# Eight small edits to the step order of a hybrid decoder layer on one core

## The chip, the core and the metric

The kernel runs on one core of a Trainium2 chip. The metric is the device time of one execution in microseconds; of several executions the median is taken. All data is float32. Matmuls run on pairs of "fp32r" tiles: every operand is split into a rounded high part and a remainder, and three products (high·high, high·low, low·high) are summed.

## What is computed

A decoder layer with five branches on 2048 tokens of width 1024, and 256 memory tokens:

```
h    = rms_norm(x, norm_g)
proj = h @ w_in                                  # (2048,1024) @ (1024,4652)
ya = spatial_gating(u, v, ...)                   # A: chunks of 128 tokens
yb = forgetting_attention(q, k, v, f, ...)       # B ("fox"): causal, QK-norm, 4 heads of 64
yc = mlstm(qk, v, i, f, o, ...)                  # C: chunkwise matrix memory, 16 chunks
yd = rwkv7_time_mix(token_shift(pd), ...)        # D: delta rule, 8 blocks of 256 tokens here
ym = memory_attention(q, rms_norm(mem) @ w_kv)   # M: cross-attention, QK-norm
out = x + concat(y * silu(z) for the five) @ w_out   # (2048,1280) @ (1280,1024)
```

## The kernel before, in words

Tokens go in four quarters of 512 (Q = 512, NQ = 4). The weight columns come in blocks of 256 (`Dk`, `Bq`, `Mq`, ...), and one block of one quarter is 48 matmuls of 512 columns or 96 of 256 columns, the three products counted. A block goes through `proj_T` (matmul line 267), `proj_T2` (line 289), `proj_tok2` (line 301) or `proj_tok` (line 315).

**Phase one** (lines 453 to 609): for each quarter the RWKV columns k, narrow, r, v, z. **Phase two** (lines 612 to 694): first the memory queries of the last quarter (`group_M`: block `Mq`, then its gate `Mz`), then for each quarter five mLSTM blocks (`Cqk0`, `Cv`, `Cqk1`, `Co`, `Cz`) and four fox blocks. **Phase three** (lines 756 to 816): blocks `Av`, `Au`, `Az`, the memory's keys and values, and `Mq`, `Mz` of the other quarters, while the attention runs beside them. **Phase four** (lines 819 to 886): the output projection by quarters (matmul line 879).

**Steps and lanes.** All work that is not a projection is written as Python generators that stop at `yield`. `tick()` (line 200) is called some eight times per block; it moves the weight loader on by a step, moves every evacuation in the crowd `evac` on by one step, and moves each of the five lanes on by its rate in steps (`RATES`, line 32: gate 0.4, mlstm 0.8, front 1.0, back 1.33, fox 1.815). `lane.drain()` and `evac.drain()` run what is left without any projection between the steps. So a `yield` more between two instructions puts one tick more, that is six matmuls of 512 columns or twelve of 256, between them in the order of the program.

The order of the program is a priority and not the order itself: a scheduler at build time lays out each engine's queue, takes the earliest instruction of the program that is ready by its own estimates, and may take later ones first where the earlier are not ready. On the chip each engine then follows its queue.

What the change touches:

- `Rwkv.front` (line 1255), one generator for each of the 8 blocks: norm and decay. It yields `2 + LATER` times (line 1316) between the reciprocal norms `rn` (DVE, `rsqrt`, lines 152 to 156) and PE's use of them (line 1322), and as often (line 1334) between the product `th` (POOL, line 1333) and its matmul (line 1338). `Rwkv.back` (line 1343) is the recurrence, one generator of 62 steps for each block, whose outcome `output` (line 1505) is stepped from the next block's `back`. A `front` waits until the output of the block before the last is out.
- `head_norm` and `qk_post` (lines 394 to 421): the QK-norm of two tiles of 128 tokens; the scaled tile `yn` (DVE, line 413) is transposed by PE (line 418) one yield later. `qk_cols` allows two of these at a time and the tile `yn` has two buffers.
- `low_rank` (line 1218): splits the low-rank weights of RWKV, with eight masks on POOL (line 1231). It is added to `evac` in quarter 0 beside block k.
- `group_M` (line 657) and the end of phase one (lines 607 to 609). The weights of the next block are fetched when a block begins (`W`, `prefetch`, `load_w`, lines 206 to 258): four tiles of 256 KB into the pool `stage["pool"]`, which is `dp` with three buffers in phase one and `sp` with two in phase two; the two pools share their memory, so that `sp` begins when `dp` is free. The lane `gate` (`gate_prep`, line 1525) gets its work at the start of phase two; it prepares the gates of branches B and C in a chain of small transfers through memory, and is drained behind `group_M`.
- `Attention.run` and `Unit` (lines 932 to 1178): 16 fox units (4 heads by 4 quarters) and 16 memory units. `maxima` finds a bound of the scores for the unit after the next; its outcome `mm` (line 1020) goes through PE (line 1069) three yields later. `average` runs `nkt` tiles of scores, exponentials `pe` (line 1087, 6 buffers) and products into `acc` (line 1108), the products three steps behind the scores, in `nkt + 3` steps. `run` spreads the steps of `maxima` over those of `average` by the ratio `per`. `finish` (line 1125) reads `acc`, which has one buffer, in the steps of the next unit.

The end of phase three in the code:

```
    while att.done < NH * (NQ + 1):
        fox.step()
    att.c5.close()
...
    while len(wo) < NK:
        load_wo()
        for _ in range(1):
            fox.step()
    fox.rate = 1.0
    for q in range(NQ):
        while att.ended < (NQ + q + 1) * NH:
            fox.step()
```

Of the kernel before, what the change touches and what calls it, by code (L numbers as in the profile page):

```python
# [18 lines left out]
P = 128  # L19
# [8 lines left out]
EPS = 1e-6  # L28
Q = 512
NQ = S // Q  # L30
LATER = 3
RATES = dict(gate=0.4, mlstm=0.8, front=1.0, back=1.33, fox=1.815)
PACE = (3, 1, 7)
EH = 0.6065306597126334
# [86 lines left out]
def body(ctx: ExitStack, tc, x, xT, mem, memT, wp, wkv, wout, pv, wa, sguT, sgub, out, dbg=None):  # L121
# [78 lines left out]
    def tick():  # L200
        step_w()
        evac.tick()
        for l in lanes.values():
            l.tick()

    def load_w(parts, src, ncol=256):

# [201 lines left out]
    def qk_post(y, scale, d):  # L409

        r = yield from head_norm(y, 512, EPS)
        y3 = y.rearrange("q (u x) -> q u x", x=HD)
        V.tensor_tensor(y3, y3, r, op=ALU.mult)
        yield
        pt = bank()
        for p in range(2):
            for ii in range(2):
                T.transpose(pt[:, (2 * p + ii) * P:(2 * p + ii + 1) * P], y[:, ii * 256 + p * P:ii * 256 + (p + 1) * P], ident)
        A.activation(y, pt, AF.Copy, scale=scale)
        yield  # L420
        SY.dma_start(d.rearrange("p q t -> q p t"), y.rearrange("q (p t) -> q p t", p=2))
# [19 lines left out]
    def tok_cols(wt, hts, i, d):  # L441


        def post(pt):
            o = xp.tile([P, 512], F32, tag="gl", name="tok")
            A.copy(o, pt)
            yield FREE
            SY.dma_start(d, o.rearrange("q (i x) -> q i x", x=256))

        evac.add(post(proj_tok(wt, hts, i)), "gl")  # L450


    with ExitStack() as c1:
# [72 lines left out]
        for q in range(NQ):  # L526
# [60 lines left out]
            for nm, j in (("k", 2), (None, 8), ("r", 0), ("v", 4), ("z", 6)):  # L587
                if not nm:
                    evac.add(narrow(proj_narrow(W("narrow"), hts), tok))
                    continue  # L590
                wt = W("D" + nm)
                if nm == "r" and q + 1 < NQ:
                    rows(q + 1, [("xt", 3)] * 3)
                pts = None
                if nm == "k" and not q:
                    pts = proj_T2(wt, hts)
                    evac.add(keep(xrs, rb0))
                    evac.add(rwkv.low_rank())
                if nm == "z":
                    pts = proj_T2(wt, hts, send(norm_x(q + 1), "norm_g", Q) if q + 1 < NQ else None)  # L600
                for p in range(2):
                    evac.add(shifted(pts[p] if pts else proj_T(wt, p, hts), j + p, (store_gate if nm == "z" else store)(dd[nm][p, :, tok])))
# [3 lines left out]
                lanes["back"].q.append(rwkv.back(2 * q + b))  # L606
        while ahead and next(ahead[-1][2], ahead) is not ahead:
            pass
        evac.drain()


    csp = cw.enter_context(ExitStack())
# [44 lines left out]
    def group_M(q, then=None):  # L657

        tok = slice(q * Q, (q + 1) * Q)
        qk_cols(W("Mq"), hts, hp2[:, 15:16], lambda i: qkd["Mq"][:, :, q * Q + i * P:q * Q + (i + 2) * P])  # L660
        wt = W("Mz")
        gate_cols(wt, hts, [gzd["M"][p, :, tok] for p in range(2)], proj_T2(wt, hts, then) if then else None)

# [225 lines left out]
class Attention:  # L889
# [42 lines left out]
    def run(self, units, ahead=2):  # L932
        mlane, flane = Lane(), Lane()
        for n in range(-ahead, len(units)):
            m = units[n + ahead] if n + ahead < len(units) else None
            if m:
                mlane.q.append(m.load())
                mlane.q.append(m.maxima())
            if n < 0:
                while mlane.q:  # L940
                    mlane.step()
                    yield
                continue
            u = units[n]
            done, per = 0, (m.nkt + 8) / (u.nkt + 3) if m else 0
            for k, _ in enumerate(u.average()):
                while done < (k + 1) * per:
                    mlane.step()
                    done += 1
                flane.step()  # L950
                self.end()
                yield
            mlane.drain()
            flane.drain()
            self.done = n + 1
            flane.q.append(u.finish())
        while flane.q or self.tails:
            flane.step()
            self.end()
            yield  # L960


class Unit:
# [66 lines left out]
    def maxima(self):  # L1030
# [31 lines left out]
        mm = fp.tile([P, 4, 4], F32R, tag="mm", name="mm")  # L1062
        A.copy(mm[:, :, 0:2], att.minus.to_broadcast([P, 4, 2]))
        self.split4(mx[:, :, 0], mm[:, :, 2:4])
        for _ in range(3):
            yield
        pm = att.bank()
        for i in range(4):
# [3 lines left out]
    def weights(self, kt):  # L1072
# [10 lines left out]
        if diag:  # L1083
            T.matmul(p2[:, f:f + P], att.identr, att.masks[0], start=False, stop=False)
        T.matmul(p2[:, f:], ka[:, ks], self.qb[:, f:], start=False, stop=True)  # L1085
        e = fp.tile([P, Q], F32, tag="pe", bufs=6, name="pe")
        A.activation(e[:, f:], p2[:, f:], AF.Exp)  # L1087
        return kt, f, e

# [20 lines left out]
    def average(self):  # L1110
        self.acc = self.att.bank("acc")
        late, pair = deque(), []
        for kt in range(self.nkt + 3):
            if kt < self.nkt:
                late.append(self.weights(kt))
            if 0 < kt <= self.nkt:
                self.rest(*late[-1 if kt == self.nkt else -2])
            if kt > 2:
                pair.append(late.popleft())
                if len(pair) == 2:  # L1120
                    self.product(pair)
                    pair = []
            yield
# [631 lines left out]
```

## Time and profile before

| what | us |
|---|---|
| median of 3 runs | 1740.68 |
| lowest of the runs | 1735.09 |
| the profiled execution, its own time | 1736.49 |
| its span, first to last instruction | 1734.8 |
| PE (TensorE, matmul) busy in the span | 1641.8 (95%) |
| DVE (VectorE) busy | 1196.9 (69%) |
| ACT (ScalarE) busy | 881.3 (51%) |
| POOL (GpSimd) busy | 302.3 (17%) |

The mean granted clock of TensorE in the span is 0.975 of full speed. PE's time is that of pipelined matmuls whose ends are modelled, so that "busy" holds slow matmuls too; idle time is the sure part. Times within the span are counted from its first instruction.

### The profile page before, as it was taken

To read this page: it belongs to the slowest core of one execution; us is meant where nothing else is said; L and a number is where in the kernel's file an instruction comes from. 1 tells how busy PE (TensorE), PEld (TensorE's weight loads), DVE (VectorE), ACT (ScalarE), POOL (GpSimd) and SP (SyncE) were. 2 spreads that over 40 slices of the span, in tenths; PEclk is the share of its full clock that TensorE was granted. 3 is DMA by queue.
4 is the path that set the end of the run, shared out by engine and by line. 5 is a ranking of instruction groups with operands and counts; after the bars stand their busy time and mean duration, and the time that the engine had idled before them with its cause. 6 is when DMAs were issued, how large, how long until landed. Compare 5 with 4: busy or idle time off the path is not lost.

```text
span 1734.8 us, 31669 instructions
## 1 busy us (share of the span) xinstructions
PE 1641.8 (95%) x11306; PEld 1282.2 (74%) x11306; DVE 1196.9 (69%) x2990; ACT 881.3 (51%) x1895; POOL 302.3 (17%) x356
## 2 busy tenths in 40 slices
PE   7898999799999999999999999999999988999999
PEld 5676778687978888798888766667656655677887
DVE  7678685685977679488676887788687786752220
ACT  5566554544555455555444756566465646631110
POOL 5010000010100101010000045344444242100000
PEclk9999999899999999999999989999999999999999
DMA  6878654542453443344334544334334425654441
GB/s 198 256 230 259 184 161 97 139 145 86 135 157 101 132 141 115 86 134 146 98 101 141 167 120 130 105 102 130 96 86 110 113 68 137 191 162 114 143 130 56
DMA packets 200151, 234.36 MB, mean 135 GB/s; under 512 B 75016, under 2 KB 107336, under 8 KB 199992
## 3 DMA queue, kind: packets, MB, share of 16 engines
q1 hardware_dynamic: 185144, 218.69, 43.7%
q10 hardware_dynamic: 14848, 13.64, 2.6%
q8 instruction: 89, 1.46, 0.4%
q14 instruction: 70, 0.57, 0.1%
HBM read 180.44 MB, written 51.81 MB: 134 GB/s over the span
## 4 chain that ended last, share of the span: by engine, by line
PE 64%; DVE 16%; DMA 11%; ACT 4%; issue 3%; POOL 1%; SPq 1%; ACTq 0%; DVEq 0%; POOLq 0%
PE pj L315 14%; PE pj L879 12%; PE pj L267 12%; PE acc L1108 4%; DMA wraw<-in_wp 4%; PE pj L289 4%; DVE wt L225 2%; PE wk L1026 2%; PE p L1082 2%; PE p L1085 2%; PE rw L1359 1%; PE rw L1482 1%; PE rw L1484 1%; DVE ht L330 1%; DVE mx L1040 1%
## 5 line engine op out<-in xcount | busy, mean ns | idle before, releaser
L267 PE MATMUL pj<-ht,wt 128*128 128x512 f32 x1632 | 422.6, 403 | 5.8 <-DVE ht L330 2.7
L267 PEld LDWEIGHTS pj<-ht,wt 128*128 128x128 f32 x1632 | 298.3, 190 | 84.5 <-issue 10.5
L315 PE MATMUL pj<-wt,ht 128*128 128x256 f32 x2400 | 332.7, 290 | 9.3 <-ACT wt L222 3.4
L315 PEld LDWEIGHTS pj<-wt,ht 128*128 128x128 f32 x2400 | 304.9, 193 | 27.5 <-issue 7.4
L225 DVE TENSOR_TENSOR wt<-wraw,wt 128x512 fp32r<-128x512 f32 (+1 forms) x312 | 217.6, 700 | 78.0 <-ACT wt L222 76.4
L222 ACT CAST wt<-wraw 128x512 fp32r<-128x512 f32 (+1 forms) x312 | 184.8, 601 | 140.2 <-DMA wraw<-in_wp 92.5
L879 PE MATMUL pj<-wo,mt 128*128 128x512 f32 x960 | 231.3, 398 | 1.8 <-ACT wo L830 1.8
L879 PEld LDWEIGHTS pj<-wo,mt 128*128 128x128 f32 x960 | 180.2, 189 | 47.2 <-issue 2.4
L1101 POOL TENSOR_TENSOR es<-es,pe 128x512 f32<-128x512 f32 (+3 forms) x128 | 153.7, 1201 | 103.9 <-ACT pe L1087 98.9
L289 PE MATMUL pj<-ht,wt 128*128 128x512 f32 x480 | 138.9, 426 | 13.3 <-ACT wt L222 11.7
L1087 ACT ACTIVATE pe<-p 128x512 f32<-128x512 f32 x192 | 100.3, 541 | 50.3 <-PE p L1085 43.9
L1040 DVE TENSOR_REDUCE mx<-wk 128x1 f32<-128x512 f32 (+3 forms) x192 | 111.8, 614 | 18.2 <-PE wk L1026 14.3
L289 PEld LDWEIGHTS pj<-ht,wt 128*128 128x128 f32 x480 | 91.8, 200 | 39.1 <-ACT wt L222 12.1
L1108 PE MATMUL acc<-pe,v 128*64 128x512 f32 (+3 forms) x384 | 104.0, 594 | 6.3 <-DVE at L1141 6.3
L329 ACT ACTIVATE ht<-xr,pvt 128x512 fp32r<-128x512 f32 (+1 forms) x88 | 61.4, 703 | 61.9 <-DMA xr<-hbd 29.2
L1099 POOL TENSOR_TENSOR es<-pe 128x512 f32<-128x512 f32 (+1 forms) x32 | 43.2, 1351 | 246.3 <-ACT pe L1087 200.3
L1026 PE MATMUL wk<-ka,qb 66*128 66x512 f32 (+3 forms) x224 | 73.2, 383 | 10.2 <-DVE mx L1040 9.7
L1082 PE MATMUL p<-qa,kb 128*128 128x512 f32 x192 | 75.8, 396 | 5.8 <-ACT pe L1087 5.8
L330 DVE SCALAR_TENSOR_TENSOR ht<-xr,pvt,ht 128x512 fp32r<-128x512 f32 (+1 forms) x88 | 68.4, 784 | 16.8 <-ACT ht L329 16.1
L859 ACT CAST mt<-mr 128x256 fp32r<-128x256 f32 x80 | 31.6, 406 | 94.1 <-DMA mr<-mix 50.3
L1026 PEld LDWEIGHTS wk<-ka,qb 66*128 66x128 f32 x224 | 41.0, 196 | 49.3 <-DVE mx L1040 19.5
L1085 PE MATMUL p<-qb,ka 68*128 68x512 f32 x192 | 75.4, 395 | 0.0
(332 smaller groups left out, 2423.1 us busy)
## 6 DMA issues: line engine op xcount, KB each, us to landing
wraw<-in_wp SPq DMA_DIRECT2D x288, 256.0 KB
xr<-hbd SPq DMA_DIRECT2D x56, 256.0 KB
mr<-mix SPq DMA_DIRECT2D x80, 128.0 KB
xr<-in_x SPq DMA_DIRECT2D x32, 256.0 KB
out<-xr ACTq DMA_DIRECT2D x32, 256.0 KB
xt<-in_x SPq DMA_DIRECT2D x24, 256.0 KB
xr<-in_xT SPq DMA_DIRECT2D x24, 256.0 KB
hbd<-xr SPq DMA_DIRECT2D x24, 256.0 KB
```

What stands on the lines that cost most here:

```text
L222: A.copy(wt[:, :, 0, :ncol], raw[:, :, :ncol])
L225: V.tensor_tensor(lo, raw[:, :, :ncol], wt[:, :, 0, :ncol].bitcast(F32), op=ALU.subtract)
L267: T.matmul(pt, wt[k // 2][:, k % 2, a, m * P:(m + 1) * P], hts[k][:, b, :], start=n == 0, stop=n == 3 * KT - 1)
L289: T.matmul(pts[m], wt[k // 2][:, k % 2, a, m * P:(m + 1) * P], hts[k][:, b, :], start=k + n == 0, stop=k == KT - 1 and n == 2)
L315: T.matmul(pt[:, ii * 256:ii * 256 + 256], hts[k][:, a, (i + ii) * P:(i + ii + 1) * P], wt[k // 2][:, k % 2, b, :], start=n == 0, stop=n = ...
L879: T.matmul(po, mts[i // 2, k][:, a, i % 2 * P:(i % 2 + 1) * P], wo[e * NK + k][:, b], start=n == 0, stop=n == 3 * NK - 1)
L1026: T.matmul(p1, self.qb[0:66, i * P:(i + 1) * P], self.k[kk][0][0:66, :w], start=True, stop=True, skip_group_check=diag)
L1040: V.tensor_reduce(*late.pop(), axis=AX.X, op=ALU.max)
L1082: T.matmul(p2[:, f:], kb[:, ks], self.qa[:, f:], start=True, stop=False)
L1085: T.matmul(p2[:, f:], ka[:, ks], self.qb[:, f:], start=False, stop=True)
L1101: G.tensor_tensor(self.sum[:, f:], self.sum[:, f:], e[:, f:], op=ALU.add)
L1108: self.att.nc.tensor.matmul(self.acc[64 * i:64 * i + 64, f:], self.v[:, kt], e[:, f:], start=kt < 2, stop=True, skip_group_check=True)
```

## The change

Before an instruction of PE that reads a norm, a maximum or an exponential, it puts one or two more steps; it gives `pe` two more buffers and corrects the ratio `per`; it adds `low_rank` two blocks later; and it runs the block `Mq` of the last quarter at the end of phase one, with the pool `dp`, while no lane is stepped.

```
-LATER = 3
+LATER = 5
...
         for l in lanes.values():
-            l.tick()
+            if not stage.get("still"):
+                l.tick()
...
         V.tensor_tensor(y3, y3, r, op=ALU.mult)
         yield
+        yield
+        yield
         pt = bank()
...
+    def group_q(q, hts):
+        qk_cols(W("Mq"), hts, hp2[:, 15:16], lambda i: qkd["Mq"][:, :, q * Q + i * P:q * Q + (i + 2) * P])
...
                     evac.add(keep(xrs, rb0))
+                if nm == "v" and not q:
                     evac.add(rwkv.low_rank())
...
         while ahead and next(ahead[-1][2], ahead) is not ahead:
             pass
+        stage["still"] = True
+        group_q(NQ - 1, hts)
         evac.drain()
+        stage["still"] = False
...
     def group_M(q, then=None):
...
-        qk_cols(W("Mq"), hts, hp2[:, 15:16], lambda i: qkd["Mq"][:, :, q * Q + i * P:q * Q + (i + 2) * P])
+        if not then:
+            group_q(q, hts)
         wt = W("Mz")
...
-            done, per = 0, (m.nkt + 8) / (u.nkt + 3) if m else 0
+            done, per = 0, (m.nkt + 9) / (u.nkt + 4) if m else 0
...
         self.split4(mx[:, :, 0], mm[:, :, 2:4])
-        for _ in range(3):
+        for _ in range(4):
             yield
         pm = att.bank()
...
-        e = fp.tile([P, Q], F32, tag="pe", bufs=6, name="pe")
+        e = fp.tile([P, Q], F32, tag="pe", bufs=8, name="pe")
...
-        for kt in range(self.nkt + 3):
+        for kt in range(self.nkt + 4):
...
-            if kt > 2:
+            if kt > 3:
                 pair.append(late.popleft())
```

## Rows read from the trace of the kernel before

**Rows 1.** Busy time by stage: stretch, length, PE PEld DVE ACT POOL, clock.

```profile
0.00:273.00 273.00, 245.23 (x1377) 189.43 (x1378) 203.53 (x507) 158.03 (x371) 39.49 (x74) 0.97 0.67 210
273.00:352.00 79.00, 68.37 (x568) 55.09 (x567) 49.38 (x132) 42.88 (x95) 4.82 (x16) 0.91 0.51 126
352.00:948.00 596.00, 582.39 (x5448) 499.16 (x5447) 442.39 (x1396) 299.21 (x664) 48.74 (x94) 1.00 0.41 120
948.00:1476.00 528.00, 494.65 (x2778) 345.23 (x2778) 405.74 (x769) 317.35 (x624) 198.24 (x164) 0.96 0.42 116
1476.00:1734.80 258.80, 251.13 (x1142) 193.28 (x1138) 95.90 (x190) 63.84 (x144) 11.05 (x8) 0.99 0.46 133
```

**Rows 2.** Whom PE waited for: total us, times, longest us.

```profile
PE wk L1069 <- DVE mm L1020: 7.1, 5, 2.0
PE acc L1108 <- DVE at L1141: 6.3, 3, 4.5
...
PE rw L1482 <- ACT qv L1476: 5.5, 1, 5.5
PE wk L1322 <- DVE rn L156: 5.1, 5, 1.5
PE wk L418 <- DVE yn L413: 3.7, 4, 1.4
PE pj L315 <- ACT wt L222: 3.4, 1, 3.4
PE wk L1338 <- POOL th L1333: 3.1, 1, 3.1
...
PE wk L494 <- POOL sq L492: 2.4, 1, 2.4
...
PE wk L418 <- DVE rq L154: 1.8, 1, 1.8
```

**Rows 3.** Timeline, 290 to 320 us: start, duration, [idle before].

```profile
297.69 1.37 SPq L211 DMA_DIRECT2D wraw<-in_wp  x2
...
307.58 0.62 ACT L222 CAST wt<-wraw 128x512 fp32r<-128x512 f32 x1 [5.89 <-DMA wraw<-in_wp]
...
308.54 1.21 PE L1482 MATMUL rw<-qv,gt 128*64 128x64 f32 x16 [5.47 <-ACT qv L1476]
```

**Rows 4.** Busy time of two stretches behind stalls, with the granted clock.

```profile
300.00:316.00 16.00, 10.53 (x66) 7.75 (x65) 5.47 (x9) 7.36 (x15) 0.74 (x1) 0.70 0.58 120
...
346.00:356.00 10.00, 8.12 (x42) 7.89 (x43) 8.43 (x25) 5.94 (x13) 1.43 (x2) 0.66 0.76 253
```

**Rows 5.** Timeline: one tick of a projection between steps of a lane.

```profile
451.83 1.69 PE L315 MATMUL pj<-wt,ht 128*128 128x256 f32 x12
```

**Rows 6.** Timeline: first and last links of the gate lane's chain.

```profile
297.10 0.48 SPq L1558 DMA_DIRECT2D mg<-gp  x1
...
310.90 0.33 SPq L1569 DMA_DIRECT2D gp<-mg  x1
...
338.28 0.33 PE L1601 MATMUL wk<-ident,gp 64*128 64x64 f32 x2
```

**Rows 7.** Timeline: RWKV's last output, and the first matmul of phase three.

```profile
928.31 1.06 ACT L1492 ACTIVATE ysq<-x 64x1024 f32<-64x1024 f32 x1
...
938.63 0.68 DVE L1518 TENSOR_TENSOR bv<-bv,zl 128x512 f32<-128x512 f32 x1
...
948.27 1.93 PE L315 MATMUL pj<-wt,ht 128*128 128x256 f32 x14 [1.77 <-DVE gz L390]
```

**Rows 8.** Timeline of PE: last projection of phase three, first of phase four.

```profile
1464.65 0.39 PE L289 MATMUL pj<-ht,wt 128*128 128x512 f32 x1
...
1476.67 2.81 PE L879 MATMUL pj<-wo,mt 128*128 128x512 f32 x6
```

**Rows 9.** Timeline of the start: POOL's masks, and a load of line 788.

```profile
10.05 7.03 POOL L1231 TENSOR_SCALAR_AFFINE_SELECT sel<-sel 32x1 f32<-32x1 f32 x8
...
14.79 0.42 SPq L788 DMA_DIRECT2D sgw<-in_sguT  x1
```

More of the change, by code (lines that the diff above doesn't have):

```diff
@@ L30 @@
 NQ = S // Q
-LATER = 3
+LATER = 5
 RATES = dict(gate=0.4, mlstm=0.8, front=1.0, back=1.33, fox=1.815)
@@ L203, in tick @@
         for l in lanes.values():
-            l.tick()
+            if not stage.get("still"):
+                l.tick()
     def load_w(parts, src, ncol=256):
@@ L414, in qk_post @@
         yield
+        yield
+        yield
         pt = bank()
@@ L450, in tok_cols, with group_q @@
         evac.add(post(proj_tok(wt, hts, i)), "gl")
+    def group_q(q, hts):
+        qk_cols(W("Mq"), hts, hp2[:, 15:16], lambda i: qkd["Mq"][:, :, q * Q + i * P:q * Q + (i + 2) * P])
     with ExitStack() as c1:
@@ L597, in body @@
                     evac.add(keep(xrs, rb0))
+                if nm == "v" and not q:
                     evac.add(rwkv.low_rank())
@@ L608, in body @@
             pass
+        stage["still"] = True
+        group_q(NQ - 1, hts)
         evac.drain()
+        stage["still"] = False
     csp = cw.enter_context(ExitStack())
@@ L659, in group_M @@
         tok = slice(q * Q, (q + 1) * Q)
-        qk_cols(W("Mq"), hts, hp2[:, 15:16], lambda i: qkd["Mq"][:, :, q * Q + i * P:q * Q + (i + 2) * P])
+        if not then:
+            group_q(q, hts)
         wt = W("Mz")
@@ L944, in run @@
             u = units[n]
-            done, per = 0, (m.nkt + 8) / (u.nkt + 3) if m else 0
+            done, per = 0, (m.nkt + 9) / (u.nkt + 4) if m else 0
             for k, _ in enumerate(u.average()):
@@ L1064, in maxima @@
         self.split4(mx[:, :, 0], mm[:, :, 2:4])
-        for _ in range(3):
+        for _ in range(4):
             yield
@@ L1085, in weights @@
         T.matmul(p2[:, f:], ka[:, ks], self.qb[:, f:], start=False, stop=True)
-        e = fp.tile([P, Q], F32, tag="pe", bufs=6, name="pe")
+        e = fp.tile([P, Q], F32, tag="pe", bufs=8, name="pe")
         A.activation(e[:, f:], p2[:, f:], AF.Exp)
@@ L1112, in average @@
         late, pair = deque(), []
-        for kt in range(self.nkt + 3):
+        for kt in range(self.nkt + 4):
             if kt < self.nkt:
@@ L1117, in average @@
                 self.rest(*late[-1 if kt == self.nkt else -2])
-            if kt > 2:
+            if kt > 3:
                 pair.append(late.popleft())
```

## The prediction, made blind

> **What bounds the kernel now.** First the busy time by stage [rows 1]. PE works all the time: the five stretches leave 27.8, 10.6, 13.6, 33.4 and 7.7 us idle, 93 of 1734.8 us. DVE, the next engine that computes, is below it in every stretch. So only two things can be won while the matmuls stay: idle time of PE, and the time in which its clock is granted at 1.2 instead of 2.4 GHz behind a gap. The clock is 1.00 in the 596 us of phase two and 0.91 and 0.96 in the two stretches with stalls; each hundredth of a stretch is that share of it in full-speed time.
>
> Second, whom PE waited for [rows 2]. The edits aim at nine of its lines: `mm` 7.1, `acc` (behind `at`) 6.3, `rn` 5.1, `yn` 3.7 and 1.8 (behind `rq`, the same norm), `th` 3.1, `sq` 2.4, and two of the turn from phase one to two, 5.5 and 3.4: together 38.4 us. None is over 5.5 us long.
>
> Third, the 5.5 in the timeline [rows 3]: the weights of `Mz` are asked for at 297.7 and are in SBUF at 307.6, since their pool begins only when phase one's is free; ACT waits with its cast, RWKV's evacuations stand behind that cast, and PE behind them. Then PE works at clock 0.70 for 16 us and, behind the 3.4, at 0.66 for 10 us [rows 4]: 4.8 and 3.4 us of full speed, of which some 2 fall on idle time, so 6 us lost.
>
> One tick of a projection is 1.69 us of PE [rows 5].
>
> **The change part by part.** It adds no matmul and no transfer: about 64 steps of generators, which cost nothing by themselves but make lanes end later. The sum is made against the profiled execution's own 1736.5 us (span 1734.8 and 1.7 around it), which lies 4 us under the median shown and 1.4 over the fastest run.
>
> *Front (LATER).* Two ticks more, 3.4 us, between `rn` and PE, and between `th` and PE. Longest waits there 1.5 and 3.1 us [rows 2]: both go, 8.2 us. Bounds: all, or nothing if the scheduler had the order wrong by more. I take 7. Each of the 8 fronts gets four ticks longer, hidden beside the 62 steps of `back` (47 ticks); only the first shows, by 4 ticks.
>
> *Norms (qk_post).* Two ticks, 3.4 us, against a longest wait of 1.8 [rows 2]: 5.5 us go. `yn`, with two buffers, is held two ticks longer, and with it may be a PSUM bank; where two such blocks follow each other a wait of up to 3.4 us can come, four times, or none, as three banks turn. I take -5.
>
> *Low rank.* POOL's masks run 7.0 us ahead of the squares that PE waits 2.4 for [rows 2, 9]. But a load of line 788, phase three, was laid out at 14.8 us [rows 9]: the scheduler fills idle engines from far ahead, so it can take the masks as early as before. Between -2.4 and +2.4; I take -1.
>
> *`Mq` in phase one.* W("Mq") now asks for `Mz`'s weights in the old pool, without a turn: the 5.5 goes. The loads of the first quarter's inputs are asked for after `Mq` instead of ahead of it, but in both orders they wait for the new pool. Against the gain, that pool begins about as late as before, and the transfers of the gate lane, which stood before `Mz`, now stand before `Cqk0` and its inputs. They made the 9.9 us of [rows 3]. So from -14.9 (both waits, 5.5 and 3.4, and the 6 of clock) to +6 (the wait comes again at `Cqk0`, with as much clock as before, and `Mz` is not faster); I take -8.
>
> *The gate lane.* Of its 8 program steps 6 came beside `Mq` and `Mz` (16 ticks at 0.4); now 3 come beside `Mz` and five are drained at one place. The row: from its first small transfer, issued at 297.1, its successor is issued only at 310.9, and the chain reaches PE at 338.3 [rows 6], 41 us, some of it behind the stall. If the scheduler reckons shorter than that, PE waits at line 1601. Nothing at best; at worst the first link's 13.8 us. I take +3, near nothing, since those transposes met no wait before.
>
> The Trainium skill (SBUF — State Buffer, "The DMA setup-cost knee") gives each transfer a roughly fixed 2 us, mostly completion. By it five links would be an estimated 10 us and be done before `Cqk0`, and this term 0; the row's first link alone, 13.8 us, disagrees with it, so I keep the chance of this wait.
>
> *RWKV's end.* I counted steps against ticks by hand: 34 ticks in each quarter of phase one, 16 of `Mq` and `Mz`, 72 in each quarter of phase two, 440 in all. The last `back` ended at tick 433. Now it starts 4 ticks later and stands still for 8: at tick 440 six steps are left and are drained uncovered. Those steps took 928.3 to 939.3, 11.0 us [rows 7]. If phase three's first matmul needs only the projection's banks, as its wait for the gate `gz` shows, nothing shows; if it needs all of PSUM or the memory of RWKV, up to 11.0. I take +3.
>
> *Maxima, products, pe.* One step more before `mm`'s use (5 waits of at most 2.0) and before `acc`'s (3, of at most 4.5): a tick is 1.69, so -5 of 7.1 and -3 of 6.3. Two more buffers of `pe` let ACT run ahead; I take -1, at most what the stage still idles. Together -9; bounds -13.4 and 0.
>
> *The fox lane's lateness.* 152 ticks at 1.815 are 275 steps in phase three. Before, unit 20, which phase four needs, ended at step 259; with one step more for each unit and two in the lead it is 281. So six steps and two of a tail stand uncovered, and the memory units of the next quarters end on ticks 176, 200 and 224, just where the quarters begin, instead of 20 and more before. The nearest row: between the last projection of phase three and the first of phase four lie 12.0 us [rows 8], fox work without cover. At best 0, since other units fill PE; at worst another 12.0 and some 3 for each of three quarters, 21. I take +5.
>
> *Clock.* The other stalls that go gave the clock gaps too: phase three at 0.96 loses 21 us of full speed. A fifth, -4; bounds 0 and -12. Against it, a new order makes waits of its own: some 55 us of idle are not aimed at (93 less 38.4); I allow under a tenth of them, +4; bounds -10 and +15.
>
> Sum: -7 -5 -1 -8 +3 +3 -9 +5 -4 +4 = -19. Each gain is taken near its bound, so I keep three quarters, -14.3: 1722.2, said as **1722.0 us**.
>
> **The rivals.**
> *The turn's wait moves on.* Gate transfers before `Cqk0`: the turn gives 0 instead of -8, and the gate lane +5: 1722 + 8 + 2 = 1732. For it: the 9.9 us transfer. Against: `Cqk0`'s inputs have all of `Mz` to come.
> *The steps do nothing.* The scheduler sorts by readiness, so one or two steps change no order where it already believed a norm was ready; the waits stay. Only the turn changes: 1736.5 - 8 + 3 + 3 = 1734 and a half. For it: the load of line 788 [rows 9]. Against: a tick of matmuls stands unbroken between steps [rows 5].
> *Slower: the fox lane comes late.* Phase four's weights go into memory that fox units hold, so it cannot begin before unit 20 ends. Six uncovered steps, a tail and three quarters cost 21; the 3 of RWKV's end stay, and gains halve to 17 of 34: 1736.5 + 21 + 3 + 3 + 4 - 17 = 1750. It decides from the point where the fox lane, not the projections, ends phase three: the first matmul of line 879 more than 12 us behind the last projection. Against: phase four has memory units as filler.
> *All of it goes*, with the clock: the gains at their bounds (-8.2, -5.5, -2.4, -14.9, -13.4, -4) and costs of 11: 1736.5 - 48.4 + 11 = 1699.
>
> **How the numbers follow.** Chances: forecast 0.42, the turn moves 0.20, nothing 0.14, slower 0.14, all 0.10. The range leaves out half of "all" and a third of "slower": 1702 to 1746; the forecast's own range is 1713 to 1730. A measurement of this kernel tells about 2% from no change, that is 1702 and 1771. Faster by over 2% is most of "all" and nothing else, 0.08; slower by over 2% needs the slower rival with RWKV's 11 us and new waits on top, 0.04; the rest, 0.88, lies within.
>
> **What would show it.** Right: the waits at lines 1322, 1338 and 418 are under 1 us each; no gap over 2 us from 273 to 352; `mm` and `acc` under 3 us each; clock over 0.96 in the turn. Wrong in a step: a wait at line 1601; at line 315 of `Av` more than the 1.8 us of [rows 7] (RWKV's end); a gap before line 879 longer than 12 us (fox lane); waits of lines 267 or 315 for `ht` or `wt` at `Cqk0` (the turn moved). The forecast is wrong if the named waits go and the span doesn't follow, or if they stay.

## The result and the profile after

The change made the kernel slower: 1769.42 us (median of 4 runs, 1763.39 to 1772.73) against 1739.89 us of the kernel before (median of 4, one of them a slow run of 2513.16 us that the ratio leaves out), ratio 1.0164 with a 95% interval of 1.0130 to 1.0197. The prediction said 1722.0 us, 1702 to 1746: the sign is wrong and the range missed it. The profiled execution of after took 1772.73 us, its span 1771.0, 36.2 more than before's 1734.8.

Busy time by stage in after, cut at the same places of the program as [rows 1]; columns: stretch, length, PE PEld DVE ACT POOL, granted clock, DMA share, GB/s:

```profile
0.00:273.00 273.00, 247.29 (x1402) 191.68 (x1403) 203.77 (x506) 158.46 (x378) 41.62 (x74) 0.97 0.69 213
273.00:352.00 79.00, 70.57 (x589) 56.01 (x588) 45.44 (x112) 38.79 (x84) 5.82 (x17) 0.91 0.50 119
352.00:966.00 614.00, 582.35 (x5404) 496.47 (x5402) 449.48 (x1419) 297.75 (x660) 48.96 (x84) 0.98 0.40 118
966.00:1495.00 529.00, 498.89 (x2713) 345.14 (x2713) 374.70 (x738) 302.97 (x595) 195.72 (x171) 0.95 0.38 108
1495.00:1771.00 276.00, 267.55 (x1204) 198.92 (x1203) 107.23 (x219) 80.50 (x179) 14.27 (x10) 0.98 0.48 136
```

Against [rows 1], phase two (third line) is 18 us longer with the same PE busy time, 582: it idles 31.7 us instead of 13.6. Phase four is 17 us longer and does 62 matmuls more (1204 against 1142); phase three does 65 fewer and is no shorter. The clock is lower in the last three stretches.

Whom PE waited for in after: total us, times, longest:

```profile
...
PE p L1093 <- ACT pe L1098: 10.3, 8, 3.4
PE wk L1037 <- DVE mx L1051: 9.5, 11, 1.6
PE rw L1526 <- DVE x L1521: 7.8, 1, 7.8
PE pj L316 <- DVE wt L226: 7.7, 4, 3.4
PE rw L1485 <- ACT xc L1479: 5.5, 2, 5.0
PE wk L1349 <- POOL th L1344: 4.2, 1, 4.2
PE wk L1080 <- DVE mm L1031: 4.0, 2, 3.2
PE acc L1119 <- DVE at L1152: 3.9, 1, 3.9
...
PE wk L1333 <- DVE rn L156: 3.7, 3, 1.5
PE wk L421 <- DVE yn L414: 3.2, 3, 1.8
PE wk L500 <- POOL sq L498: 3.0, 1, 3.0
```

And two rows of the same view of before, which the rows ahead of the prediction don't hold:

```profile
PE wk L1026 <- DVE mx L1040: 9.7, 10, 3.2
...
PE p L1082 <- ACT pe L1087: 5.8, 5, 2.3
```

The waits that the edits aimed at went in part and came back beside: `mm` 7.1 to 4.0 and `at` 6.3 to 3.9, but `pe` 5.8 to 10.3, while `mx`, the maxima's own wait, stayed (9.7 and 9.5); `rn` 5.1 to 3.7, but `th` 3.1 to 4.2 and `sq` 2.4 to 3.0. Two are new: 7.8 us at RWKV's last transposes, and 7.7 in four places at line 316, where a projection waited for DVE's half of its weights (`wt`; before lost 0.9 to that, at line 267). No run isolates what brought the second.

The turn from phase one to two, timeline of after, which answers [rows 3]:

```profile
297.32 0.33 SPq L634 DMA_DIRECT2D xr<-hbd  x1
...
306.87 0.72 ACT L330 ACTIVATE ht<-xr,pvt 128x512 fp32r<-128x512 f32 x1 [7.20 <-DMA xr<-hbd]
...
307.81 0.26 ACT L1479 COPY xc<-rw 64x128 f32<-64x128 f32 x1
...
308.12 0.98 PE L1485 MATMUL rw<-xc,x 64*64 64x64 f32 x8 [5.04 <-ACT xc L1479]
```

This is the same stall with another load: not `Mz`'s weights but the first inputs of `Cqk0` are asked for at 297.3, ACT waits 7.20 for them, RWKV's evacuation stands behind ACT's wait, and PE waits 5.04 instead of 5.47. The idle time of the second stretch fell from 10.6 to 8.4 us, its clock stayed 0.91.

The end of phase two, timeline of PE in after, which answers [rows 7], and three stretches around it:

```profile
955.16 1.20 PE L268 MATMUL pj<-ht,wt 128*128 128x512 f32 x4
964.11 1.08 PE L1526 MATMUL rw<-ident,x 64*128 64x64 f32 x8 [7.75 <-DVE x L1521]
966.25 5.97 PE L316 MATMUL pj<-wt,ht 128*128 128x256 f32 x30 [1.06 <-DVE bv L1528]
```

```profile
944.00:956.00 12.00, 12.00 (x115) 8.69 (x114) 4.86 (x9) 4.74 (x13) 0.00 (x0) 1.00 0.39 132
956.00:966.00 10.00, 1.44 (x10) 0.92 (x8) 7.10 (x19) 2.63 (x4) 0.00 (x0) 0.74 0.31 105
966.00:972.00 6.00, 5.75 (x30) 5.78 (x31) 0.80 (x2) 2.18 (x7) 1.26 (x9) 0.57 0.30 87
```

The last projection of phase two ends at 956.4; RWKV's last output stands behind it with nothing to cover it, and `Av` waits for it. PE works 1.4 of 10 us, and its clock is granted at 0.74 there and 0.57 in the next 6.

The end of phase three in after, which answers [rows 8]:

```profile
1474.79 0.86 PE L290 MATMUL pj<-ht,wt 128*128 128x512 f32 x3
...
1491.07 1.97 PE L1119 MATMUL acc<-pe,v 128*64 128x512 f32 x2 [3.94 <-DVE at L1152]
...
1498.54 0.79 PE L890 MATMUL pj<-wo,mt 128*128 128x512 f32 x1 [0.67 <-ACT mt L870]
```

From the end of the last projection to the output projection lie 22.9 us instead of 11.6 [rows 8], fox work alone.

So the span's 36.2 us add up at four marks. The first matmul of `Av` is 18.0 later (948.27 to 966.25); from there to the end of the last projection of phase three it is 7.4 less (516.8 to 509.4); then 11.3 more to line 890; then 14.3 more to the end (258.1 to 272.5). The 3600th projection matmul, late in phase two, began at 931.1 before and at 931.4 after, but that is no draw. Up to there PE idled 57.2 us in after and 50.0 in before, and after had done 160 fewer of RWKV's matmuls (2296 against 2456). It does them beside the last projections of the phase, with PE busy throughout. So of the 18.0 us by which `Av` is later, some 9.6 are that work (931.4 to 956.4, against 931.1 to 946.5), and 8.1 are the longer stall (9.9 against 1.8).

### The profile page after: what moved, and what is told of

The parts are those of the page before. It is cut to its first block, busy times and chain, and to the rows that moved or that the text cites. A ratio compares the mean times of both kernels' runs of the same rounds, so it can differ in the third digit from the quotient of the medians.

```text
span 1771.0 us, 31667 instructions
## 1 busy us (share of the span) xinstructions
PE 1666.7 (94%) x11306; PEld 1288.2 (73%) x11306; DVE 1180.6 (67%) x2990; ACT 878.5 (50%) x1895; POOL 306.4 (17%) x356
## 4 chain that ended last, share of the span: by engine, by line
PE 53%; DVE 19%; DMA 15%; ACT 6%; issue 4%; SPq 1%; POOL 1%; ACTq 0%; DVEq 0%; POOLq 0%
PE pj L268 12%; PE pj L890 10%; PE pj L316 9%; DMA wraw<-in_wp 5%; PE acc L1119 4%; DVE wt L226 3%; PE pj L290 2%; DMA xr<-hbd 2%; PE wk L1037 2%; PE p L1093 2%; PE p L1096 2%; DVE rq L154 1%; DVE xtmp L1417 1%; DMA xr<-in_xT 1%; DVE mx L1051 1%
## 5 line engine op out<-in xcount | busy, mean ns | idle before, releaser
L268 PEld LDWEIGHTS pj<-ht,wt 128*128 128x128 f32 x1632 | 302.6, 193 | 86.5 <-issue 11.7
L316 PE MATMUL pj<-wt,ht 128*128 128x256 f32 x2400 | 336.2, 293 | 12.5 <-DVE wt L226 7.7
L316 PEld LDWEIGHTS pj<-wt,ht 128*128 128x128 f32 x2400 | 308.7, 196 | 33.1 <-issue 10.1
L226 DVE TENSOR_TENSOR wt<-wraw,wt 128x512 fp32r<-128x512 f32 (+1 forms) x312 | 223.6, 720 | 84.7 <-ACT wt L223 83.7
L890 PE MATMUL pj<-wo,mt 128*128 128x512 f32 x960 | 238.6, 402 | 1.2 <-ACT mt L870 1.0
L290 PEld LDWEIGHTS pj<-ht,wt 128*128 128x128 f32 x480 | 88.8, 195 | 40.2 <-ACT wt L223 11.6
L1119 PE MATMUL acc<-pe,v 128*64 128x512 f32 (+3 forms) x384 | 109.9, 582 | 3.9 <-DVE at L1152 3.9
L1093 PE MATMUL p<-qa,kb 128*128 128x512 f32 x192 | 77.0, 401 | 10.3 <-ACT pe L1098 10.3
L870 ACT CAST mt<-mr 128x256 fp32r<-128x256 f32 x80 | 31.7, 405 | 84.7 <-DMA mr<-mix 69.3
```

What stands on the lines that cost most here:

```text
L226: V.tensor_tensor(lo, raw[:, :, :ncol], wt[:, :, 0, :ncol].bitcast(F32), op=ALU.subtract)
L268: T.matmul(pt, wt[k // 2][:, k % 2, a, m * P:(m + 1) * P], hts[k][:, b, :], start=n == 0, stop=n == 3 * KT - 1)
L290: T.matmul(pts[m], wt[k // 2][:, k % 2, a, m * P:(m + 1) * P], hts[k][:, b, :], start=k + n == 0, stop=k == KT - 1 and n == 2)
L316: T.matmul(pt[:, ii * 256:ii * 256 + 256], hts[k][:, a, (i + ii) * P:(i + ii + 1) * P], wt[k // 2][:, k % 2, b, :], start=n == 0, stop=n = ...
L890: T.matmul(po, mts[i // 2, k][:, a, i % 2 * P:(i % 2 + 1) * P], wo[e * NK + k][:, b], start=n == 0, stop=n == 3 * NK - 1)
L1093: T.matmul(p2[:, f:], kb[:, ks], self.qa[:, f:], start=True, stop=False)
```

## The experiments

The theory was lateness: what a lane does later in program order stands uncovered where its stage ends, for RWKV at the end of phase two (eight ticks without a lane), for the fox lane at phase four. The rivals were that the edits themselves cost, and that any new order is a new lot. Ratios are to the kernel before on the same chip, with 95% intervals; "turn" below is the time between the 720th and the 1440th projection matmul, counted in program order (idle PE and full-speed time lost to the clock in it), and `Av`, phase three, gap and phase four are cut at the marks above, from starts.

```
run                 ratio   turn (idle, clock)   Av     three  gap   four
before              1       200.5 (12.4,  8.5)   948.3  516.4  12.0  258.1
after               1.0164  196.9 (14.9,  7.5)   966.3  509.0  23.3  272.5
a1 lanes go on      1.0027  204.0 (11.6, 17.1)   958.6  504.1  22.4  272.2
a4 back 1.36        1.0021  200.5 (16.1,  8.5)   958.8  500.0  24.0  271.5
a2 fox as before    1.0107  193.3 (13.8,  3.8)   980.8  525.1  12.0  262.9
b1 block, stand     1.0066  195.7 (14.4,  3.4)   970.1  515.6  12.0  258.7
b2 block alone      0.9965  196.6 (12.2,  6.8)   946.7  517.6  12.0  259.8
b3 attention alone  1.0070  204.2 (13.1, 13.7)   949.3  512.4  23.0  268.9
c3 product alone    1.0016  203.4 (12.1, 13.7)   948.9  499.0  18.8  272.5
c4 maxima alone     1.0114  202.7 (12.4, 11.9)   949.6  519.7  16.8  265.0
c1 norms alone      1.0094  211.4 (16.8, 20.5)   965.0  522.4  12.0  259.2
d2 LATER 5 alone    1.0123  209.5 (17.2, 17.1)   966.2  522.4  12.0  259.5
e1 LATER 4 alone    1.0100  214.6 (18.9, 20.5)   973.6  522.9  12.0  259.8
b4 block, norms     0.9994  199.0 (12.0, 10.2)   950.0  515.7  12.0  258.8
```

The columns come from one execution each, in six sessions: the kernel before had a median of 1739.9 us beside after, 1750.9 beside a1 to a4, 1748.5 beside b1, b2, b3 and b5, 1742.1 beside b4 and the c runs, 1740.4 beside the d runs and 1749.4 beside the e runs. So two rows of different sessions can differ by some 10 us for that alone; the ratios are free of it. b4 and a1 are the same program up to phase three, and their `Av` differ by 8.6 us. Five kernels that equal before up to there (before, b3, c3, c4, and d1 below at 946.2) lie within 3.4; in the turn they run from 200.5 to 204.2 us, with 8.5 to 13.7 lost to the clock, and before is the lowest in both. a2's profiled execution, 1782.6 us, is 13 above its own median.

**Lanes standing still, from the changed kernel.**

```diff
-        stage["still"] = True
+        stage["still"] = False
         group_q(NQ - 1, hts)
```

> The kernel after, but the lanes go on beside the memory queries' block, which stays in phase one. Theory 'lateness' (the edits make the RWKV lane and the fox lane end later in the order of the program, and the end of phase two and phase four pay for it): RWKV's last output comes out at tick 437 of 440 instead of six steps behind it; the 20 us lost between the last fox block of phase two and the first block of phase three shrink to under 6, and the 20 us won at the turn, which were only put off, shrink as much without a net loss: 1753, against 1769 of the kernel after. Rival 'the edits themselves' (the added steps hold tiles and banks longer, and that costs): 1766 to 1772. Rival 'a new order is a new lot' (each edit lays the queues anew and the sum is chance): anywhere from 1750 to 1785, with the losses at other places than these two.

Measured 1.0027 [0.9997, 1.0057]: 1.4 of the 1.6 per cent gone. The other cure keeps the lanes standing and lets RWKV's `back` run faster:

```diff
-RATES = dict(gate=0.4, mlstm=0.8, front=1.0, back=1.33, fox=1.815)
+RATES = dict(gate=0.4, mlstm=0.8, front=1.0, back=1.36, fox=1.815)
```

> The kernel after with the rate of RWKV's back lane 1.36 instead of 1.33, so that its last output is out at tick 437 of 440 although the lanes stand still for eight; all edits stay. Lateness: the 20 us between phases two and three shrink to under 6, 1753. The edits themselves: 1766 to 1772. A new lot: 1750 to 1785.

Measured 1.0021 [0.9999, 1.0043]. Timeline of PE at the end of phase two, with the lanes going on:

```profile
951.67 0.68 PE L1526 MATMUL rw<-ident,x 64*128 64x64 f32 x8 [0.94 <-DVE x L1521]
952.29 4.85 PE L268 MATMUL pj<-ht,wt 128*128 128x512 f32 x20
958.59 1.69 PE L316 MATMUL pj<-wt,ht 128*128 128x256 f32 x12 [1.46 <-DVE gz L391]
```

and with the rate up:

```profile
951.86 0.68 PE L1526 MATMUL rw<-ident,x 64*128 64x64 f32 x8 [0.95 <-DVE x L1521]
...
958.77 10.94 PE L316 MATMUL pj<-wt,ht 128*128 128x256 f32 x89 [1.46 <-DVE gz L391]
```

In both the last output has projections behind it again, the 7.75 is under 1, and `Av` waits for the gate `gz` as it did before the change. Both reach the 3600th projection matmul 7.6 us later than after does (939 against 931.4), having done more lane work by then (2424 of RWKV's matmuls against 2296), and the 4080th, early in phase three, 15 us sooner (1093 against 1109): all that their spans win, 13.6 and 16.7 us, is won between these two marks. The part from the end of phase two's last projection to the 4080th, in after, a1 and a4:

```profile
956.36:1108.50 152.14, 133.21 (x732) 98.53 (x733) 112.74 (x239) 90.10 (x178) 41.98 (x43) 0.91 0.46 133
```

```profile
957.13:1093.10 135.97, 127.28 (x725) 93.09 (x725) 108.54 (x224) 89.87 (x177) 44.32 (x43) 0.97 0.54 152
```

```profile
957.31:1093.60 136.29, 128.73 (x726) 93.30 (x726) 107.90 (x224) 90.00 (x177) 44.71 (x43) 0.96 0.56 152
```

But for the 8 matmuls of the stalled output, the three have the same matmuls there. After idles 18.9 us against 8.7 and 7.6, of which 8.4 are the longer stall, and loses 13.7 us of full-speed time to the clock against 3.4 and 5.1.

The control, the same rate on the kernel before:

> The kernel before with back's rate at 1.36 in place of 1.33 and nothing else, as a control. RWKV ended seven ticks before phase two's end, so lateness expects nothing of it: 1.000 within 0.003. If the rate is a gain by itself, so that its cure of the changed kernel says nothing of lateness: 0.994 or less.

1.0036 [1.0012, 1.0060]: no gain by itself, a small loss even, a little outside the 0.003 allowed. So what the rate wins in the changed kernel is not a gain that it brings anywhere.

**The block with and without standing still, from the kernel before.** b1 takes these lines over from the change, with `group_q`, the test in `tick()` and `group_M` as changed; b2 is the same with `False`.

```diff
+        stage["still"] = True
+        group_q(NQ - 1, hts)
         evac.drain()
+        stage["still"] = False
```

> The kernel before with one part of the change alone: the memory queries' block at the end of phase one, the lanes standing still beside it; LATER is 3, and norms and attention are as before. Lateness (eight ticks without a lane come back as RWKV work at the end of phase two, with one step left at the last tick, 440, where the whole change has six): half of the change's loss, ratio 1.004 to 1.010, and a wait at the transposes of x at the end of phase two that lasts longer than before's. Rival, it takes the standing still and LATER together: ratio 1.000 (within 0.003), no such wait. Rival, standing still costs by itself, whatever is left: 1.012 or more. In all three the projections reach the same place at the turn about 18 us earlier than before (number 960) and have given that back 80 us later.

> The kernel before with the memory queries' block at the end of phase one, the lanes going on beside it. My prediction's term for the turn says -8 us from this alone, ratio 0.995. The turn's-wait-moves-on theory (the wait of 5.5 us for RWKV's first matmuls and the loads of the next weights meet PE later): ratio 1.000 within 0.003, with the same idle time between 273 and 400 us as before's within 3 us. Lateness says nothing against either, since the lanes keep their ticks.

b1: 1.0066 [1.0038, 1.0095]; b2: 0.9965 [0.9936, 0.9994]. One word costs 1.0 per cent. Timeline of PE at the end of phase two in b1:

```profile
967.96 0.68 PE L1523 MATMUL rw<-ident,x 64*128 64x64 f32 x8 [1.90 <-DVE x L1518]
970.07 13.24 PE L316 MATMUL pj<-wt,ht 128*128 128x256 f32 x96 [1.42 <-DVE bv L1525]
```

and in b2:

```profile
934.39 0.68 PE L1523 MATMUL rw<-ident,x 64*128 64x64 f32 x8 [0.49 <-DVE x L1518]
946.73 7.82 PE L316 MATMUL pj<-wt,ht 128*128 128x256 f32 x63 [1.77 <-DVE gz L391]
```

The stall is small in b1, where one step is left at the last tick and not six: 4.0 us without a projection against 1.8 in b2. Of the 20.2 us by which b1's span is longer, 9.1 lie between the 3600th and the 4080th projection matmul, where the theory puts the loss; 12.5 lie between the 2640th and the 2880th, where the clock fell (last section); of those the theory says nothing. The block alone was run again:

> The block at the end of phase one with the lanes going on, once more. If it is faster than the kernel before: 0.994 to 0.998 again with the interval below 1. If the first measurement was luck: 1.000.

0.9972 [0.9953, 0.9991]: a gain of some 0.3 per cent, the only part of the change that was measured as one, and a kernel faster than both. (The two yields and the low rank's place were not run by themselves.) In b2 the stall is still at the turn, 5.83 us, at another line of RWKV (1399) behind ACT, whose cast before that waits for weights.

**Attention.** The four edits undone in the changed kernel (a2, below as a diff of after), done alone in the kernel before (b3, the same lines the other way), and the fox rate raised in the changed kernel (a3, `fox=1.815` to `1.969`):

```diff
-            done, per = 0, (m.nkt + 9) / (u.nkt + 4) if m else 0
+            done, per = 0, (m.nkt + 8) / (u.nkt + 3) if m else 0
...
-        for _ in range(4):
+        for _ in range(3):
...
-        e = fp.tile([P, Q], F32, tag="pe", bufs=8, name="pe")
+        e = fp.tile([P, Q], F32, tag="pe", bufs=6, name="pe")
...
-        for kt in range(self.nkt + 4):
+        for kt in range(self.nkt + 3):
...
-            if kt > 3:
+            if kt > 2:
```

> The kernel after with the four edits of the attention undone (three yields behind the maxima, products three steps behind, six buffers, the old ratio). Lateness: the 17 us lost in phase four (line 890) go, phase three stays as it is: 1752. The edits themselves: also about 1752, but with phase three 5 us faster or more. A new lot: no part of it is bound to come back, 1750 to 1785.

> The kernel before with the four attention edits alone (a fourth step at the maxima, products one tile later, eight buffers pe, the share of memory steps). Fox lateness (some 86 of the lane's matmuls pass from phase three to phase four, where each costs its full time, while phase three, with fewer of them, stays as long): ratio 1.004 to 1.008, phase four about 15 us longer. My prediction's gains at the maxima and the products: ratio 0.997 or less. Rival, the edits cost only beside the other parts: 1.000 within 0.003.

> The kernel after with the fox lane's rate 1.969 instead of 1.815, so that unit 20 ends at tick 143 of phase three, as before the change; all edits stay. Lateness: phase four wins its 17 us back, 1753. The edits themselves: nothing comes back, 1766 to 1772. A new lot: 1750 to 1785.

Undone 1.0107 [1.0062, 1.0151], alone 1.0070 [1.0043, 1.0098], rate up 1.0127 [1.0098, 1.0156]. The gap ahead of the output projection is 22 to 24 us in every kernel with the four edits at the old rate, and 11.3 to 12.0 in every kernel with none of them. Its ends in b3 and in a2:

```profile
1460.45 1.66 PE L289 MATMUL pj<-ht,wt 128*128 128x512 f32 x6
1484.68 1.65 PE L879 MATMUL pj<-wo,mt 128*128 128x512 f32 x3 [0.68 <-ACT mt L859]
```

```profile
1504.85 1.42 PE L290 MATMUL pj<-ht,wt 128*128 128x512 f32 x5
1517.90 2.29 PE L890 MATMUL pj<-wo,mt 128*128 128x512 f32 x5
```

The rate hardly helps, a miss for the theory, which had 1753: against after the gap (19.8) and phase four (268.1) are 7.9 us shorter together, but phase three (516.8) is 7.8 longer.

Then the edits apart, in the kernel before. c3 has the first, third, fourth and fifth of these lines as changed; c4 only the second; d1 is c4 with the share raised:

```diff
-            done, per = 0, (m.nkt + 8) / (u.nkt + 3) if m else 0
+            done, per = 0, (m.nkt + 9) / (u.nkt + 3) if m else 0
```

> The kernel before with the products one tile later, eight buffers pe and the memory steps' share that goes with it. Counted by hand, each of the lane's units takes one step more and phase three ends with 19 units done in place of 23; so fox lateness expects nearly the whole loss of the attention edits here: ratio 1.004 to 1.008, phase four 12 us longer or more. Rival, the loss comes from the step at the maxima or from the buffers' traffic: 1.000 within 0.003.

> The kernel before with the fourth step at the maxima alone. Counted by hand, the step falls beside others that the lane takes anyway: 22 units done at the end of phase three in place of 23, and the lane ends two steps later in all. Lateness expects no loss: ratio 0.997 to 1.002. My prediction's gain at the maxima (the waits for mm and mx) would give 0.996. Rival, the step costs by itself as the products' does: 1.003 or more.

> The kernel before with the fourth step at the maxima and the memory steps' share raised by one, so that one step is left at each unit's end as before. If the loss of the step alone came from the two steps run together at each unit's end: ratio within 0.003 of 1.000, with the waits for mx and mm back near 9.7 and 7.1 us. If the step itself costs (the maxima's order against the other lanes and the projections): 1.006 or more, waits for mx above 13 us. My prediction's gain would give 0.996.

c3: 1.0016 [0.9989, 1.0043], a miss for the theory's ratio and a hit for its phase four: 14.4 us longer and a gap of 18.8, as counted, but phase three 17.4 shorter. Being late moves the work and here costs nothing that the interval shows. c3 is also the one run in which the waits fell together (`mm` 3.9, `at` 2.8, `pe` 4.8, in sum 11.5 against 19.2 before), and no time is won by it. c4: 1.0114 [1.0067, 1.0160], a miss: no lateness by the count, and the largest loss of the attention edits. The count was off too: c4's gap is 4.8 us longer than before's and its phase four 6.9, 11.7 of the 16.3 us by which its span is longer. PE's waits in c4:

```profile
PE wk L1026 <- DVE mx L1040: 16.4, 17, 2.5
PE p L1082 <- ACT pe L1087: 10.5, 8, 3.4
PE wk L1069 <- DVE mm L1020: 8.3, 8, 2.3
```

The step that was to shorten `mm`'s wait left it at 8.3 and raised those of `pe` and `mx`. With its share (d1) it costs 1.0034 [1.0018, 1.0051], `mm` 4.8, `mx` 11.5 and `pe` 15.4. So the step trades one wait for the next in the lane and is paid for even in its better form; without the share, which by the count by hand leaves two of its steps to run together at each unit's end, it costs more. The share without the step (d1's diff), on top of the block alone (b2), was the try for a better kernel, d4:

> The kernel before with the memory queries' block at the end of phase one, the lanes going on (alone 0.9965), and the memory steps' share raised by one, so that no step is left at a unit's end. If steps run together at the unit's end make PE wait for mx and mm: 0.992 to 0.995, faster than both kernels, with these waits below 9.9 and 5.2 us. If they do not: 0.9965 within 0.003.

1.0010 [0.9987, 1.0033]: no gain, less than the block alone, and neither of the two values expected.

**Upstream.** LATER 5, the two yields and the low rank's place, done alone in the kernel before (c1):

```diff
-LATER = 3
+LATER = 5
...
         yield
+        yield
+        yield
         pt = bank()
...
                     evac.add(keep(xrs, rb0))
+                if nm == "v" and not q:
                     evac.add(rwkv.low_rank())
```

> The kernel before with the three edits upstream alone: LATER 5, the two steps in front of the transposes of the normalized queries and keys, and the low rank's products one block later. My prediction's terms for them are -7, -5 and -1 us, three quarters of it kept: ratio 0.994. Lateness adds four ticks to RWKV's end, which still lies inside phase two: no cost. Rival, the waits go only in part or come back at the next instruction: ratio 0.998 to 1.001, with the waits at the transposes behind rn and yn falling by less than half of their 5.1 and 3.7 us.

1.0094 [1.0061, 1.0127], a miss both for lateness and for my terms. Then the first line by itself, LATER at 5 (d2) and at 4 (e1):

> The kernel before with LATER 5 in place of 3 and nothing else. If the loss of the upstream edits (1.0094) is that of the first RWKV block's norms reaching the turn later, where there is too little other work to cover it: 1.005 to 1.010, with the extra time between the projections 960 and 1200 (before: 57.7 us for this stretch) and a lower granted clock there. If it is that of the two steps at the normalized queries and keys or the low rank's place: 1.000 within 0.003. My prediction's term (-7 us) would give 0.996.

> The kernel before with LATER 4 in place of 3. If what LATER costs at the turn grows with the steps added (two steps of the front lane for each unit of LATER): about half of 1.0123, 1.004 to 1.008, with half of the extra time between the projections 960 and 1200. If the loss is that of a new order of the program, not of lateness: anything else, 1.000 or again 1.012.

1.0123 [1.0099, 1.0147] and 1.0100 [1.0079, 1.0120]. The place was as expected only in part. The turn is 9 to 14 us longer than before's in all three, with 9 to 12 us more lost to the clock; against the four other kernels with before's program there (b3, c3, c4, d1) that is 5 to 12 us, with 3 to 9 lost to the clock. Their spans are 24 to 34 us longer than before's, so about half of the loss or less lies in the turn. Two stretches of the turn in e1:

```profile
300.00:345.00 45.00, 38.15 (x170) 28.98 (x169) 22.17 (x50) 17.86 (x34) 1.80 (x5) 0.70 0.40 82
345.00:380.00 35.00, 27.58 (x156) 24.68 (x156) 24.69 (x72) 15.49 (x32) 6.26 (x9) 0.80 0.59 168
```

The same two in before:

```profile
300.00:345.00 45.00, 37.25 (x214) 28.64 (x212) 28.93 (x78) 22.46 (x45) 2.96 (x7) 0.89 0.50 124
345.00:380.00 35.00, 31.86 (x199) 29.08 (x200) 32.66 (x93) 18.40 (x35) 7.10 (x8) 0.90 0.49 154
```

PE is as busy as before in the first stretch, but gets through 170 matmuls instead of 214. It is not a slope: one unit of LATER costs as much as two. By the test set for e1 that speaks against lateness and for a new order of the program.

**Both cures together.** b5 is the changed kernel with the diffs of a4 and a2, b4 with those of a1 and a2.

> The changed kernel with back's rate at 1.36 in place of 1.33 and the attention edits undone: what is left is LATER, the two yields, the low rank's place, and the block with the lanes standing still. If the two latenesses are separate and add, the losses of 1.4 and 0.5 per cent both go and what is left is the gain of the edits upstream: ratio 0.994 to 0.999, faster than both kernels. If they are one loss seen twice: 1.002, as with the rate alone.

> The changed kernel with the lanes going on beside the block and the attention edits undone: both sources of lateness gone, what is left are the edits upstream and the block's place. If those two add: the block alone measured 0.9965, the edits upstream give 0.994 to 1.000, so 0.991 to 0.997, the fastest kernel of this study. If the change has a loss that neither lateness explains: 1.000 or more.

0.9990 [0.9970, 1.0009] and 0.9994 [0.9973, 1.0015]. The two losses are separate and both are gone, but no gain of the upstream edits is left: b4 is b2 plus those edits, 0.9994 against 0.9965. With the block ahead of the turn they cost some 0.3 per cent, without it 0.9 (c1; LATER alone 1.0 to 1.2); c1 and b4 differ in the block's place alone.

## Why the prediction was wrong, step by step

**RWKV's end, +3 with bounds of 0 to 11: the step that failed most.** The count was right: the lane had seven ticks of slack, stood still for eight and started four later, and its last steps came behind the last projection. The price was wrong. I asked only whether `Av` needs those steps, and took the value near nothing; after's row shows `Av` waiting behind `bv`, RWKV's last output, with 9.9 us without a projection. The stall alone lies inside the bound of 11. What the term left out is the clock behind it, granted at 0.74 and 0.57: up to the 4080th projection matmul after loses 13.7 us of full-speed time, the two cures 3.4 and 5.1 (before, with other attention work there, 10.2). Letting the lanes go on, or speeding RWKV's up, wins 1.4 per cent, some 24 us by the ratios and 14 to 17 in the profiles, all of it between the end of phase two and early phase three; the profiles show less, since the kernel before was 11 us slower, too, in the cures' session (1750.9 against 1739.9). So the upper bound was too low.

**The fox lane's lateness, +5 with bounds of 0 to 21.** The rival "the fox lane comes late" had the mechanism and the place that I named: a gap ahead of the output projection of more than 12 us (22.9), and it had a chance of only 0.14. What was not in it: the work that leaves phase three makes that phase shorter (c3: 17.4 us), so lateness by itself is not shown to be the loss. Net, the four edits cost 0.3 to 0.7 per cent in four pairs (after and a2, b3 and before, a1 and b4, a4 and b5).

**Maxima, products, pe: -9.** Of these three waits of the attention lane, 19.2 us before (7.1, 6.3, 5.8), 18.2 stayed in after (4.0, 3.9, 10.3). That is no accident of one profile: with the four edits at the old rate the sum is 16.7 to 19.9 (after, a1, a4, b3), without them 16.8 to 20.6 (before, a2, b4, b5). The step sized each wait by itself; a later maximum hands its wait to the exponentials (`pe` 10.5 in c4 and 15.4 in d1, at a loss in both). With the products alone later (c3) the sum did fall, and still no time was won.

**Front -7 and norms -5.** "Both go" failed: `rn` kept 3.7 of 5.1 and `th` rose to 4.2. For `yn` 3.2 of 3.7 stayed; only the wait behind `rq`, 1.8, is no longer at line 421. And the sentence "only the first shows, by 4 ticks" gave that delay no price, while LATER alone costs 1.0 to 1.2 per cent, about half of it or less at the turn; whether by that delay is open (e1). With the block ahead of the turn some two thirds of what the three edits cost are gone (b4 and b2 against c1).

**`Mq` in phase one, -8.** Beside a lane that goes on, the block is worth 0.3 per cent, 5 to 6 us: sign right, size near. But the size is luck. The rival "the turn's wait moves on" is what the timeline shows, with 5.04 of the 5.47 us back at `Cqk0`'s inputs, and 5.83 in b2; where the block's gain comes from instead, no run shows.

**Low rank -1, gate lane +3, clock -4, new waits +4.** `sq` went from 2.4 to 3.0 us: nothing. The gate lane's transposes (line 1612) met no wait in after: nothing. The 13.8 us of [rows 6] were misread: SyncE's queue, which issues the transfers in turn, stood from 301.6 to 308.95 at a load of weights (6.0 us of it until the weights asked for before had landed), and the next link stood behind it. The row does not show that a small transfer took long. The clock's sign was wrong: 0.975 before, 0.966 after over the whole span, 17 us of full-speed time out of 36 ((1 - 0.966) x 1771.0 less (1 - 0.975) x 1734.8; after's other executions had 0.967 to 0.974). The waits that were not aimed at grew by far more than 4: PE's idle time rose from 93.0 to 104.4 us, although those aimed at fell from 38.4 to some 30. And three quarters were kept of the whole sum, costs included; of the gains alone they would have left -10.5 and 1726.

**The single cause above these.** I priced delays by the waits they shorten and let the uncovered ends cost almost nothing. The runs show the opposite: of the six gains only the block's showed, and the two ends, RWKV's 1.4 and the fox lane's and its maxima's 0.3 to 0.7 per cent, make up the whole loss of 1.6: with both mended 0.9990 and 0.9994 are left. How the second splits into lateness and the maxima's step is not shown.

What stays open: why one unit of LATER costs as much as two, and whether that is the lateness of the first front or, as e1 suggests, a new order alone; how far the maxima's loss in the changed kernel is that of c4 or of d1; and why phase three is 6 us longer in the two kernels with LATER alone (d2, e1), whose phase three is the same program.

## What to carry to other kernels

Count for every lane how many ticks it has left at its stage's end; when a change takes more than that, price the end as a stall (the steps, the wait of the next stage on them, and the clock behind them), not as the steps alone. Where several waits lie in one chain of a lane, the sum of them is the number to watch: delaying one stage can move the wait to the next, and even a smaller sum is no gain until the whole has been timed. And a stage's end that merely moves work into the next stage is no loss until both stages have been timed.

## What the runs showed of the hardware

In two kernels with the lanes standing still the clock fell with hardly a stall ahead of it. Three stretches of a2, in which PE's only listed wait is 1.0 us, at line 1456:

```profile
700.00:720.00 20.00, 20.00 (x170) 16.36 (x168) 14.45 (x38) 6.67 (x13) 2.64 (x1) 1.00 0.53 141
720.00:740.00 20.00, 19.03 (x165) 13.19 (x165) 5.88 (x16) 7.27 (x23) 0.64 (x1) 0.53 0.22 65
740.00:760.00 20.00, 20.00 (x180) 14.99 (x180) 8.81 (x24) 9.32 (x27) 0.64 (x1) 0.78 0.27 84
```

and one of b1, whose program is there between the same two projection matmuls, 2640 and 2880:

```profile
718.00:746.00 28.00, 28.00 (x191) 19.65 (x189) 8.87 (x23) 8.93 (x28) 1.71 (x2) 0.51 0.21 67
```

PE is busy nearly all the time, and some 27 us are granted at the lower of the two levels, 13.7 us lost. In a2 PE ran mostly matmuls of 64 by 128 and of 32 by 32 in the 4 us before the fall; after, with the same program there, runs the same ones and keeps 1.00. a2's other three executions were 12 to 14 us shorter, about what the fall costs, so it need not come in each. No run here explains it.
